# Attention's scores moved to earlier steps, and five of eight units per layer turned by DMA into the room of their own probabilities

## The chip, the core and the metric

The kernel runs on one core of one Trainium2 chip. A core has five engines with a queue of instructions each: PE (matrix products), ACT (activation functions, copies and casts), DVE (elementwise work and reductions), POOL, and SP, which here issues transfers. An instruction starts when those ahead of it in its queue have started and the semaphores that it waits for have come. Transfers run on 16 DMA engines. The metric is the device time of one execution in microseconds (us), as a median of runs.

## The reference

A trunk of two layers over 512 positions of width 1024, in float32. Each layer is a gated feed-forward (inner width 2816), a mixing stage, and a second feed-forward; a last norm follows. The change lies in the mixing stage:

```python
h = rms_norm(x, mix_norm[l])
z = h @ w_in[l]                                   # -> q | k | v | conv_B | conv_C | conv_h
attn_out = sliding_window_attention(q, k, v, attn_sink[l])
conv_out = short_conv(conv_B, conv_C, conv_h, conv_w[l])
x = x + jnp.concatenate([attn_out, conv_out], axis=-1) @ w_out[l]
```

Attention has 8 query heads of 64 in two groups that share a key and a value head. A block of 128 queries sees its own block of keys and the one before; a distance bias is added, and each head has a learned sink:

```python
scores = scores + bias[None, None]
scores = jnp.where(mask_b, scores, -jnp.inf)
m = jnp.maximum(jnp.max(scores, axis=-1, keepdims=True), sink_l)
p = jnp.where(mask_b, jnp.exp(scores - m), 0.0)
denom = jnp.sum(p, axis=-1, keepdims=True) + jnp.exp(sink_l - m)
out = jnp.einsum("bnkgqs,bnskd->bnqkgd", (p / denom), v_band)
```

## The kernel before

**Float32 by halves.** A float32 operand is split into a high and a low part (`hi`, `lo`): ACT casts the number to a shorter format, DVE subtracts that from the number. A product is three PE passes: high by high, low by high, high by low (L314 to L317). Feed-forward and output projection use a scheme with seven products in place of eight (`Seven`, matmuls at L941).

**Weights.** They come in pieces of 128x1024 (`raw`, eight rooms), loaded by SP's queue (L206), some with further pieces added to them by POOL's (L217, L278). ACT casts `wh` (L222) and DVE subtracts `wl` (L223), each with four rooms, three pieces ahead of PE (`SPLIT_AHEAD`); the load is called for four pieces ahead of the split (`LOAD_AHEAD`).

**The mixing stage.** Keys, values and the first two heads of `q` come from three products in halves of the positions (L350). Then fifteen whole products of 24 matmuls follow, each 128 columns of `w_in` by all 512 positions: three for `q` (two heads each), twelve for the convolution. `attend(step)` is called behind each one: the step is `2 + j` in the loop over `q`, so that step 3 is behind the first whole product, and goes on to 17 in `go_on`. In it, stages of attention stand that the tables at the top of the kernel give to this step.

**Attention's units.** There are eight per layer: block n of 4 by group g of 2, in the tables in the order (0,0), (1,0), (2,0), (3,0), (0,1), (1,1), (2,1), (3,1). A unit has four heads, and goes through these stages:

- `scores` (L1544, L1545 on PE; DVE adds the bias and takes the maximum, L1548; ACT takes the exponential, L1565, with the sink's in `es`, L1568; DVE scales by the sum, L1573). `p` is 128 queries by 4 x 256 keys, in a room of the weights' eight (`stock`). Units of n = 0 have only 128 keys.
- The probabilities must be turned, keys to partitions. `turn` does it on PE, four 128x128 transposes per block of keys (L1623), split from PSUM by ACT (L1626) and DVE (L1627).
- The other way is by DMA, for a unit with an entry in `SEND_AT`. DMA turns 16-bit elements, so `apart` has ACT copy the upper and the lower 16 bits of `p` into two planes (L1588, two copies of 128x1024), `send` has SP turn each plane (L1595), and `join` has ACT put the halves together again (L1608, two copies); ACT and DVE then split as above (L1612, L1614). Before, this is the way of units (1,0), (3,0) and (1,1), and `join` writes into `p` from a room of four planes, in `g8` or `xf`.
- `values` (L1638, L1639): PE multiplies by the values `vv`; ACT copies the upper half of the partitions (`ol`, L1641) and DVE adds the two into `mixed[0]` (L1644).

**Order.** A scheduler of the language places each engine's instructions by its own estimates of time. What it does to the order stands in the program: each engine runs its list as it is, and PE can't pass an instruction that waits. The rooms (`raw` 8, `g8` 4, `xf` 8, `g2` 11, PSUM `sc` 2, `aux` 2, `mm` 4) are reused as they come free, and a later user waits for the last reader.

Of the kernel before, what the change touches and what calls it, by code (L numbers as in the profile page):

```python
# [8 lines left out]
F32 = mybir.dt.float32  # L9
# [3 lines left out]
U16 = mybir.dt.uint16  # L13
# [3 lines left out]
P = 128  # L17
# [7 lines left out]
KC = D // P  # L25
NT = S // P
# [14 lines left out]
LAST = INNER[:-1] + (("d", (9, 10)),)  # L41
FORMS = ("a11", "a12", "s2", "s3", "s1", "a22", "s4")
EARLY = ("a11", "a12", "s3", "s2", "a22", "s1", "s4")
SCORES_AT = (5, 6, 7, 8, 9, 10, 12, 13)
TURN_AT = (6, None, 8, None, 11, None, 14, 15)
SEND_AT = (None, 7, None, 9, None, 11, None, None)
JOIN_AT = (None, None, None, None, None, 14, None, None)
LATE_JOIN_AT = (None, 10, None, 12, None, None, None, None)
VALUES_AT = (7, 11, 9, 13, 12, 15, 15, 16)
WARM = 3  # L50
XT_TAGS = ("sc", "aux", "aux", "mm", "sc", "sc", "aux", "aux")

# [24 lines left out]
def trunk_kernel(  # L77
# [23 lines left out]
    nc = tc.nc  # L101
# [3 lines left out]
    xpool = ctx.enter_context(tc.tile_pool(name="xpool", bufs=1))  # L105
# [7 lines left out]
    def g2(name, dt=F32, shape=(P, S)):  # L113
        return work.tile(list(shape), dt, tag="g2", bufs=11, name=name)

    def g8(name, dt=F32R, shape=(P, 2, 2, S)):
        return work.tile(list(shape), dt, tag="g8", bufs=4, name=name)
# [23 lines left out]
    def f32(ap):  # L141
        return ap.bitcast(F32)
# [576 lines left out]
    class Seven:  # L719
# [7 lines left out]
        def make(self, *names):  # L727
            for what in names:
                if what in self.forms:
                    continue  # L730
                hi, lo = both(f"f{what}_{self.name}")
                self.forms[what] = (hi, lo)
                b11, b12, b21, b22 = (
                    self.full[j][:, :, t * H : (t + 1) * H] for j in range(2) for t in range(2)
                )
                if what in ("t2", "t3") and not self.sums:
                    self.sums = self.room(self.name)
                    nc.vector.tensor_sub(self.sums[0], b12, b22)
# [748 lines left out]
    def mix(l, norm, after):  # L1487
        q = [None] * NH
# [35 lines left out]
        class Unit:  # L1524


            def __init__(self, n, g):
                self.n, self.g = n, g
                self.far = SEND_AT[NT * g + n]
                self.name = f"{l}_{n}_{g}"  # L1530
# [45 lines left out]

            def apart(self):

                if n_of(self) % NT == 1:
                    self.room = g8(f"pr_{self.name}", U16, (P, 4, KC * P))  # L1580
                else:
                    self.room = xpool.tile(
                        [P, 4, KC * P], U16, tag="xf", bufs=8, name=f"pr_{self.name}"
                    )
                src = self.p.bitcast(U16).rearrange("p h (b k z) -> p z h b k", b=2, z=2)
                with tc.issue_after(state["cast"].ins):
                    for z in range(2):
                        nc.scalar.copy(  # L1588
                            self.room[:, z].rearrange("p (b h k) -> p h b k", b=2, h=4), src[:, z]
                        )  # L1590

            def send(self):
                with tc.issue_after(state["load"].ins):
                    for z in range(2):
                        nc.sync.dma_start_transpose(  # L1595
                            self.room[:, 2 + z].rearrange("p (g q) -> p g q", q=P), self.room[:, z]
                        )

            def join(self):

                dst = self.p.bitcast(U16).rearrange("p h (k z) -> p z (h k)", z=2)
                turned = self.p.rearrange("p h k -> p (h k)").rearrange(
                    "p (b h q) -> p b h q", b=2, h=4
                )
                self.pt = []
                with tc.issue_after(state["cast"].ins):
                    for z in range(2):
                        nc.scalar.copy(dst[:, z], self.room[:, 2 + z])  # L1608
                for kb in range(2):
                    hi = g2(f"ph_{self.name}_{kb}", F32R, (P, 4, P))  # L1610
                    lo = g2(f"pl_{self.name}_{kb}", F32R, (P, 4, P))
                    nc.scalar.copy(hi, turned[:, kb])  # L1612
                    with tc.issue_after(state["sub"].ins):
                        nc.vector.tensor_sub(lo, turned[:, kb], f32(hi))  # L1614
                    self.pt.append((kb, hi, lo))
# [31 lines left out]

        todo = [Unit(n, g) for g in range(NKV) for n in range(NT)]

        def n_of(unit):  # L1650
            return NT * unit.g + unit.n

        def attend(step, what=(VALUES_AT, JOIN_AT, TURN_AT, SEND_AT, SCORES_AT)):

            stages = {VALUES_AT: "values", TURN_AT: "turn", SEND_AT: "send", SCORES_AT: "scores"}
            done = None
            for at in what:
                for unit, own in zip(todo, at):
                    if own == step:
                        done = getattr(unit, stages.get(at, "join"))() or done  # L1660
            return done

        for j in range(NH // 2):
# [3 lines left out]
            if j % 2 == 0:  # L1667
                room = both(f"q_{l}_{j}", shape=(P, 2, 2, S))
# [10 lines left out]
        step = 6  # L1679
# [4 lines left out]
        def go_on():  # L1684

            nonlocal step
            last = attend(step)
            step += 1
            with tc.issue_after(last.ins) if last else nullcontext():
                need_split(state["group"] - 1 + SPLIT_AHEAD)  # L1690
            attend(step - 1, (LATE_JOIN_AT,))

        for pair in range(2):
            cs = []
# [73 lines left out]
```

## Time and profile before

| | |
|---|---|
| median of 3 runs | 1641.39 us (1641.3 to 1644.91) |
| profiled execution | 1641.66 us, its span 1639.9 us |
| PE busy | 1629.8 us, 99% of the span |
| DVE, ACT, POOL busy | 1300.8, 1128.7, 193.5 us |
| mixing stage of layer 1, first whole product to first product of the output projection | 358.76 to 459.23 us |
| the 64 transposes of `p` on PE (L1623) | 270 to 329 ns each, the median 272 |

How to read it: times are from the start of the span. A row of the timeline gives start, duration, engine, line, operation, what is written and read, shape and count; in brackets the idle time before it and who ended it. Matmuls are pipelined, so the distance from one start to the next tells what a matmul takes of PE, and its duration, which is longer, does not. A row of the groups gives busy time and mean nanoseconds of one, then the idle time before. In a row of the windows, each engine's busy time in that stretch stands with its count of instructions.

### The profile page before, as it was taken

The page shows a single profiled execution, that of the slowest core. Times are in us where ns is not written, and L with a number is a line of the kernel's source. Part 1 is how long each engine was busy: PE and PEld are TensorE (multiplying, and loading weights), DVE is VectorE, ACT ScalarE, POOL GpSimd, SP SyncE. Part 2 cuts the span into 40 slices and gives each one's busy share as a digit, 9 for nine tenths or more (in the row PEclk, how much of TensorE's full clock was granted, in tenths as well). Part 3 has the DMA queues.
Part 4 walks back from the last instruction along what each step waited for, and adds up shares of the span by engine and source line. Part 5 has one row for each costly group of instructions (what it writes and reads, how often), then busy time and mean ns, then how long its engine had stood idle before and what let it go on. Part 6 is the DMA issues. An engine that isn't in the chain of part 4 may idle for free.

```text
span 1639.9 us, 21080 instructions
## 1 busy us (share of the span) xinstructions
PE 1629.8 (99%) x7576; PEld 1356.7 (83%) x7576; DVE 1300.8 (79%) x1718; ACT 1128.7 (69%) x1581; POOL 193.5 (12%) x172
## 2 busy tenths in 40 slices
PE   9999999999999999999999999999999999999998
PEld 7888888888888888888888888888988888888886
DVE  7987779877799867798788677896578987768895
ACT  7457777556867667786576777865587775777864
POOL 0011111100111111112001111110002101111111
PEclk9999999999999999999999999999999999999999
DMA  9379999932685788999837898996137857999991
GB/s 257 86 196 219 225 215 256 221 93 58 167 205 129 205 205 206 218 228 248 231 78 204 207 218 220 232 250 194 53 90 167 208 131 191 213 224 223 227 263 65
DMA packets 286844, 308.64 MB, mean 188 GB/s; under 512 B 108532, under 2 KB 171028, under 8 KB 286740
## 3 DMA queue, kind: packets, MB, share of 16 engines
q1 hardware_dynamic: 244212, 227.99, 47.8%
q0 software_dynamic: 41824, 78.65, 28.1%
q8 instruction: 59, 0.97, 0.2%
q10 hardware_dynamic: 704, 0.66, 0.1%
q14 instruction: 45, 0.37, 0.1%
HBM read 263.74 MB, written 2.10 MB: 162 GB/s over the span
## 4 chain that ended last, share of the span: by engine, by line
PE 92%; DVE 4%; ACT 1%; DMA 1%; issue 1%; SPq 0%; ACTq 0%; DVEq 0%
PE x L941 25%; PE y L941 13%; PE x_s L941 10%; PE w L941 6%; PE y_s L941 5%; PE down L373 3%; PE acc L314 3%; PE acc L315 3%; PE acc L317 3%; PE up L1097 3%; PE w_s L941 3%; PE acc L350 2%; DVE wl L223 1%; PE acc L839 1%; DMA raw<-in_w_out_dram 1%
## 5 line engine op out<-in xcount | busy, mean ns | idle before, releaser
L223 DVE TENSOR_TENSOR wl<-raw,wh 128x1024 fp32r<-128x1024 f32 (+1 forms) x493 | 596.2, 1214 | 219.9 <-ACT wh L222 216.7
L222 ACT CAST wh<-raw 128x1024 fp32r<-128x1024 f32 (+1 forms) x493 | 513.2, 1046 | 312.2 <-PE y L941 41.6
L941 PE MATMUL y<-wh,ft 128*128 128x512 f32 x608 | 187.3, 389 | 0.0
L941 PE MATMUL x<-wh,fb 128*128 128x512 f32 x608 | 187.3, 389 | 0.0
L941 PE MATMUL x<-wh,ft 128*128 128x512 f32 x608 | 187.3, 389 | 0.0
L941 PEld LDWEIGHTS x<-wh,ft 128*128 128x128 f32 x608 | 114.1, 188 | 23.7
L941 PEld LDWEIGHTS x<-wh,fb 128*128 128x128 f32 x608 | 114.1, 188 | 23.7
L941 PEld LDWEIGHTS y<-wh,ft 128*128 128x128 f32 x608 | 114.1, 188 | 23.7
L941 PE MATMUL y<-wl,ft 128*128 128x512 f32 x304 | 118.3, 389 | 0.0
L941 PE MATMUL x<-wl,fb 128*128 128x512 f32 x304 | 118.3, 389 | 0.0
L941 PE MATMUL x<-wl,ft 128*128 128x512 f32 x304 | 118.3, 389 | 0.0
L217 POOL DMA_DIRECT2D raw<-in_ffn_wu_dram x39 | 47.3, 1222 | 544.3 <-DMA raw<-in_ffn_wu_dram 327.0
L1266 ACT COPY raw_a<-pt 128x1024 uint16<-128x1024 uint16 x76 | 103.2, 1358 | 11.1 <-DMA pt<-pl 11.1
L314 PE MATMUL acc<-hh,wh 128*128 128x512 f32 x240 | 94.7, 394 | 0.0
L315 PE MATMUL acc<-hl,wh 128*128 128x512 f32 x240 | 93.8, 391 | 0.0
L317 PE MATMUL acc<-hh,wl 128*128 128x512 f32 x240 | 93.7, 391 | 0.0
L941 PE MATMUL w<-wh,fb 128*128 128x512 f32 x304 | 93.6, 389 | 0.0
L941 PE MATMUL x_s<-wh,ft_s 128*128 128x512 f32 x256 | 78.8, 389 | 0.0
L941 PE MATMUL y_s<-wh,ft_s 128*128 128x512 f32 x256 | 78.8, 389 | 0.0
L250 DVE TENSOR_TENSOR raw<-raw,raw 128x1024 f32<-128x1024 f32 x58 | 70.6, 1222 | 7.1 <-DMA raw<-in_ffn_wd_dram 5.9
L217 POOL DMA_DIRECT2D raw<-in_ffn_wg_dram x39 | 47.1, 1212 | 233.7 <-DVE u L1250 62.3
L941 PE MATMUL x_s<-wh,fb_s 128*128 128x512 f32 x240 | 73.9, 389 | 0.0
(364 smaller groups left out, 3421.3 us busy)
## 6 DMA issues: line engine op xcount, KB each, us to landing
raw<-in_ffn_wu_dram SPq DMA_DIRECT2D x120, 512.0 KB, 5.2
raw<-in_ffn_wd_dram SPq DMA_DIRECT2D x104, 512.0 KB, 6.3
raw<-in_ffn_wg_dram SPq DMA_DIRECT2D x80, 512.0 KB, 4.9
raw<-in_ffn_wu_dram POOLq DMA_DIRECT2D x39, 512.0 KB, 8.1
raw<-in_ffn_wg_dram POOLq DMA_DIRECT2D x39, 512.0 KB, 6.0
raw<-in_w_in_dram SPq DMA_DIRECT2D x36, 512.0 KB, 4.3
raw<-in_ffn_wd_dram POOLq DMA_DIRECT2D x32, 512.0 KB, 8.5
raw<-raw POOLq DMA_DIRECT2D x20, 512.0 KB, 8.5
```

What stands on the lines that cost most here:

```text
L217: nc.gpsimd.dma_start(out=r, in_=rows_of(*more), accum_op=ALU.add)
L222: cast = nc.scalar.copy(hi, raw)
L223: state["sub"] = eng.tensor_sub(lo, raw, f32(hi))
L250: nc.vector.tensor_add(a11, a11, s1)
L314: nc.tensor.matmul(acc, hi[:, k, :], rhs[k][0], start=k == first, stop=False)
L315: nc.tensor.matmul(acc, hi[:, k, :], rhs[k][1], start=False, stop=False)
L317: nc.tensor.matmul(acc, lo[:, k, :], rhs[k][0], start=False, stop=k == last)
L350: nc.tensor.matmul(accs[j][:, t * H : (t + 1) * H], w[:, k, :], x_, start=t + k + i == 0, stop=k == KC - 1 and i == 2, skip_group_check=True,)
L373: nc.tensor.matmul(acc, a[:, k, tok], w[:, k, :], start=i + k + n == 0 and fresh[t], stop=i == last and k == 1 and n == 2, skip_group_chec ...
L941: nc.tensor.matmul(accs[u], x_[:, 2 * h + k, tok], w[:, k, :], start=start and h + k + i == 0, stop=h + k == 2 and i == 2, skip_group_chec ...
L1097: nc.tensor.matmul(accs[t], x_[:, tok], w[:, k, :], start=j + k + i == 0, stop=j == 3 and k == 1 and i == 2,)
L1266: nc.scalar.copy(room.rearrange("p c (n z) -> p c z n", z=2)[:, :, z, :], turned[0][:, NT * z + 2 * c : NT * z + 2 * c + 2, :],)
```

## The change

Two things change, in the same way in both layers.

**When.** Scores move from steps 5, 6, 7, 8, 9, 10, 12, 13 to 3, 4, 5, 6, 8, 7, 9, 11, so that unit (1,1) now goes ahead of (0,1). Turning, sending, joining and `values` move with them. There is one table for `join` in place of two, and a join stands behind the call for the next weight split of its step.

**How.** Units (2,0) and (2,1) also go by DMA, so that only (0,0), (0,1) and (3,1) are turned on PE. The four planes become two (`planes`): `apart` writes into them, `send` turns them into the room of `p` itself (`back`), and `join` writes from there into the planes, where the split then reads. Four units share two rooms by halves, one of `g8` and one of `xf`; the fifth takes a room of the weights' eight.

```diff
-SCORES_AT = (5, 6, 7, 8, 9, 10, 12, 13)
-TURN_AT = (6, None, 8, None, 11, None, 14, 15)
-SEND_AT = (None, 7, None, 9, None, 11, None, None)
-JOIN_AT = (None, None, None, None, None, 14, None, None)
-LATE_JOIN_AT = (None, 10, None, 12, None, None, None, None)
-VALUES_AT = (7, 11, 9, 13, 12, 15, 15, 16)
+SCORES_AT = (3, 4, 5, 6, 8, 7, 9, 11)
+TURN_AT = (4, None, None, None, 10, None, None, 13)
+SEND_AT = (None, 5, 6, 7, None, 8, 10, None)
+JOIN_AT = (None, 8, 9, 10, None, 11, 13, None)
+VALUES_AT = (6, 9, 10, 11, 12, 12, 14, 15)
...
             def apart(self):
-                if n_of(self) % NT == 1:
-                    self.room = g8(f"pr_{self.name}", U16, (P, 4, KC * P))
-                else:
-                    self.room = xpool.tile(
-                        [P, 4, KC * P], U16, tag="xf", bufs=8, name=f"pr_{self.name}"
-                    )
                 src = self.p.bitcast(U16).rearrange("p h (b k z) -> p z h b k", b=2, z=2)
+                self.planes = rooms.pop(0)()
                 with tc.issue_after(state["cast"].ins):
                     for z in range(2):
                         nc.scalar.copy(
-                            self.room[:, z].rearrange("p (b h k) -> p h b k", b=2, h=4), src[:, z]
+                            self.planes[:, z].rearrange("p (b h k) -> p h b k", b=2, h=4), src[:, z]
                         )
             def send(self):
+                self.back = self.p.rearrange("p h k -> p (h k)").bitcast(U16)
+                self.back = self.back.rearrange("p (z n) -> p z n", z=2)
                 with tc.issue_after(state["load"].ins):
                     for z in range(2):
                         nc.sync.dma_start_transpose(
-                            self.room[:, 2 + z].rearrange("p (g q) -> p g q", q=P), self.room[:, z]
+                            self.back[:, z].rearrange("p (g q) -> p g q", q=P), self.planes[:, z]
                         )
             def join(self):
-                dst = self.p.bitcast(U16).rearrange("p h (k z) -> p z (h k)", z=2)
+                whole_ = self.planes.rearrange("p z n -> p (z n)")
+                dst = whole_.rearrange("p (n z) -> p z n", z=2)
+                turned = whole_.bitcast(F32).rearrange("p (b h q) -> p b h q", b=2, h=4)
                 self.pt = []
                 with tc.issue_after(state["cast"].ins):
                     for z in range(2):
-                        nc.scalar.copy(dst[:, z], self.room[:, 2 + z])
+                        nc.scalar.copy(dst[:, z], self.back[:, z])
...
+        rooms = [half_of(f"pr_{l}_0", h, in_g8) for h in range(2)]
+        rooms += [half_of(f"pr_{l}_1", h, in_xf) for h in range(2)]
+        rooms.append(lambda: stock(f"pr_{l}_2", U16, (P, 2, KC * P)))
...
-            attend(step - 1, (LATE_JOIN_AT,))
+            attend(step - 1, (JOIN_AT,))
```

The order that the scheduler then gives, in the same way in both layers. On PE the scores of unit (0,0) stand behind and within the first two whole products, its transposes within the third; the output products of (1,0), (2,0) and (3,0) stand ahead of and among the matmuls of the eighth, ninth and tenth. On ACT the copies that part, the copies that join and the casts of five units lie between the third product and the end of the eleventh, with the casts of the weights between them. On SP the turns of a unit stand between the loads of `w_in`, as before, now five pairs in place of three.

More of the change, by code (lines that the diff above doesn't have):

```diff
@@ L1595, in send @@
                         nc.sync.dma_start_transpose(
-                            self.room[:, 2 + z].rearrange("p (g q) -> p g q", q=P), self.room[:, z]
+                            self.back[:, z].rearrange("p (g q) -> p g q", q=P), self.planes[:, z]
                         )
             def join(self):
-                dst = self.p.bitcast(U16).rearrange("p h (k z) -> p z (h k)", z=2)
-                turned = self.p.rearrange("p h k -> p (h k)").rearrange(
-                    "p (b h q) -> p b h q", b=2, h=4
-                )
+                whole_ = self.planes.rearrange("p z n -> p (z n)")
+                dst = whole_.rearrange("p (n z) -> p z n", z=2)
+                turned = whole_.bitcast(F32).rearrange("p (b h q) -> p b h q", b=2, h=4)
                 self.pt = []
@@ L1648, in mix, with half_of, room, in_g8 @@
         todo = [Unit(n, g) for g in range(NKV) for n in range(NT)]
-        def n_of(unit):
-            return NT * unit.g + unit.n
-        def attend(step, what=(VALUES_AT, JOIN_AT, TURN_AT, SEND_AT, SCORES_AT)):
+        shared_rooms = {}
+        def half_of(name, half, make):
+            def room():
+                if not half:
+                    shared_rooms[name] = make(name)
+                return shared_rooms[name][:, half]
+            return room
+        def in_g8(name):
+            return g8(name, U16, (P, 2, 2, KC * P))
+        def in_xf(name):
+            return xpool.tile([P, 2, 2, KC * P], U16, tag="xf", bufs=8, name=name)
+        rooms = [half_of(f"pr_{l}_0", h, in_g8) for h in range(2)]
+        rooms += [half_of(f"pr_{l}_1", h, in_xf) for h in range(2)]
+        rooms.append(lambda: stock(f"pr_{l}_2", U16, (P, 2, KC * P)))
+        def attend(step, what=(VALUES_AT, TURN_AT, SEND_AT, SCORES_AT)):
             stages = {VALUES_AT: "values", TURN_AT: "turn", SEND_AT: "send", SCORES_AT: "scores"}
```

## The prediction

> **What bounds the kernel now.** I read the page first, then the waits of the output products of attention, then the mixing stage of layer 1 cut into windows, then its groups by shape and its timeline.
>
> ```profile
> PE 1629.8 (99%) x7576; PEld 1356.7 (83%) x7576; DVE 1300.8 (79%) x1718; ACT 1128.7 (69%) x1581; POOL 193.5 (12%) x172
> ...
> PE 92%; DVE 4%; ACT 1%; DMA 1%; issue 1%; SPq 0%; ACTq 0%; DVEq 0%
> ...
>   DVE pl L1627: 1.0, 2
>   DVE pl L1614: 0.4, 2
> ...
> core 0: us, PE busy (x) PEld busy (x) DVE busy (x) ACT busy (x) POOL busy (x), PEclk, DMA share, GB/s
> 358.76:377.00 18.24, 18.24 (x89) 15.27 (x88) 9.96 (x13) 11.80 (x18) 0.00 (x0) 1.00 0.20 58
> 377.00:390.00 13.00, 13.00 (x67) 10.77 (x66) 10.67 (x38) 9.01 (x26) 0.00 (x0) 1.00 0.15 42
> 390.00:405.00 15.00, 15.00 (x82) 12.69 (x81) 12.04 (x36) 10.51 (x22) 1.29 (x1) 1.00 0.39 93
> 405.00:420.00 15.00, 15.00 (x73) 12.52 (x73) 11.85 (x46) 14.66 (x37) 1.30 (x1) 1.00 0.47 117
> 420.00:435.00 15.00, 15.00 (x75) 12.56 (x74) 11.36 (x31) 14.66 (x25) 1.22 (x1) 1.00 0.59 144
> 435.00:447.00 12.00, 12.00 (x64) 10.09 (x62) 9.86 (x23) 7.53 (x17) 2.78 (x2) 1.00 0.74 168
> 447.00:459.23 12.23, 12.18 (x56) 9.77 (x54) 10.69 (x16) 6.11 (x10) 3.69 (x3) 1.00 0.91 217
> ```
>
> PE is busy for 99% of the span and carries 92% of the chain, so the time changes in two ways only: PE gets less to do, or PE is made to wait. In attention the output products' second halves (L1639) are what PE still waits at: 1.4 us in four places of two layers, for DVE. The windows show what covers the rest: ACT, off the chain over the whole run, is full from 405 to 435 (14.66 of 15.00, twice) and has spare time before and behind. This is where the change puts more on ACT. Layer 2 runs the same instructions in the same order, so I work one layer and double it.
>
> **What PE is spared.** Two more units per layer (unit 2 of both groups of heads) are turned by DMA, so 2 x 8 transposes leave PE; units (0,0), (0,1) and (3,1) keep 4 + 4 + 8.
>
> ```profile
> 358.76 0.40 PE L314 MATMUL acc<-hh,wh 128*128 128x512 f32 x1
> ...
> 430.63 0.39 PE L1638 MATMUL o<-ph,vv 128*128 128x512 f32 x1
> ...
> 431.62 0.28 PE L1544 MATMUL sc<-k,q 128*128 128x256 f32 x1
> ...
> 432.58 0.40 PE L314 MATMUL acc<-hh,wh 128*128 128x512 f32 x1
> ...
> 438.05 1.04 PE L1623 MATMUL pt<-ident,p 128*128 128x128 f32 x8
> 438.85 0.48 PE L314 MATMUL acc<-hh,wh 128*128 128x512 f32 x1
> ...
> 452.99 0.39 PE L1638 MATMUL o<-ph,vv 128*128 128x512 f32 x1
> 453.43 0.50 PE L1639 MATMUL o<-pl,vv 128*128 128x512 f32 x1
> 453.76 0.40 PE L314 MATMUL acc<-hh,wh 128*128 128x512 f32 x1
> ```
>
> The pitch counts, not the duration: eight transposes take 438.85 - 438.05 = 0.80 us and hold up the next matmul some 0.1, so 16 of them are 1.8 us. A whole product (24 matmuls) takes 438.05 - 432.58 = 5.47, 0.228 a matmul; a unit's scores 432.58 - 431.62 = 0.96 (0.9 for unit 0, whose are half as wide); four output matmuls 431.62 - 430.63 = 0.99. The waits at L1639 delay PE by less than their 0.7 a layer: at the last one the matmuls stand 0.44 and 0.33 apart in place of 0.23, 0.3 lost, some 0.4 with the other. Those halves now come earlier, so that goes too. In all 2.2 us a layer are spared: 4.4 in the program, if nothing else happened.
>
> The Trainium skill (VectorE: DVE Perf Modes, "The three transpose paths") gives a 128x128 transpose 390 ns on TensorE and 1309 ns by the DMA crossbar, and under its rules says to use TensorE where PSUM will do as destination, which speaks against this change. Taken as PE's price, 390 ns would make the spared 16 an estimated 6.2 us a layer in place of 1.8; the pitch of 0.10 above decides.
>
> **What ACT gets in exchange.** For each of the two units: two copies that part the halves (L1588), two that join them (L1608), and two casts from SBUF (L1612) in place of two from PSUM (L1626).
>
> ```profile
> L222 ACT CAST wh<-raw 128x1024 fp32r<-128x1024 f32 x16 | 16.8, 1052 | 14.1 <-PE acc L315 14.1
> L1608 ACT COPY p<-pr 128x1024 uint16<-128x1024 uint16 x6 | 7.9, 1361 | 0.0
> L1588 ACT COPY pr<-p 128x1024 uint16<-128x1024 uint16 x6 | 6.0, 1045 | 0.0
> L1626 ACT CAST ph<-pt 128x512 fp32r<-128x512 f32 x8 | 4.5, 589 | 1.1 <-PE pt L1623 1.1
> L1612 ACT CAST ph<-p 128x512 fp32r<-128x512 f32 x6 | 3.5, 622 | 0.0
> L1706 ACT ACTIVATE cc<-ch,par 128x512 f32<-128x512 f32 x4 | 2.9, 723 | 1.7 <-DVE ch L1704 1.7
> ...
> 391.17 2.00 ACT L1588 COPY pr<-p 128x1024 uint16<-128x1024 uint16 x2
> 393.07 0.51 ACT L1565 ACTIVATE p<-p,nm 128x256 f32<-128x256 f32 x1
> ...
> 395.05 0.20 ACT L1568 ACTIVATE es<-es 128x4 f32<-128x4 f32 x1
> ...
> 411.16 0.40 ACT L1565 ACTIVATE p<-p,nm 128x128 f32<-128x128 f32 x1
> ...
> 412.71 0.20 ACT L1568 ACTIVATE es<-es 128x4 f32<-128x4 f32 x1
> ...
> 422.44 2.59 ACT L1608 COPY p<-pr 128x1024 uint16<-128x1024 uint16 x2
> 424.89 1.05 ACT L222 CAST wh<-raw 128x1024 fp32r<-128x1024 f32 x1
> ```
>
> Back to back, ACT's instructions overlap by about 0.1: a pair that parts is 1.90, a pair that joins 2.45, a unit's exponentials with `es` 2.08 (1.65 for unit 0), a weight cast 0.95, a 512-wide cast or copy 0.50, `cc` and `tap` together 1.26. So ACT gets 2 x (1.90 + 2.45) = 8.7 us a layer on 74.28 of 100.47 (the windows summed): 83 of 98. On average it has room; what counts is where.
>
> The Trainium skill (ScalarE: Activation LUTs, "What ACT_TABLE_LOAD costs") has ACT take one element per cycle at any width, 186 + 0.833 N ns: an estimated 1039 ns for both copies. The parting copy agrees (1045), the joining one does not (1361), and the row decides.
>
> **Where PE meets ACT.** The fifteen whole products of the stage are P1 (358.76) to P15; step k follows P(k-2). Scores now follow P1 to P7 and P9; the output products of units (1,0), (2,0), (3,0) follow P7, P8 and P9, and stand in PE's order among the matmuls of P8 to P10. PE cannot pass them.
>
> *After P1.* Unit 0's scores need all of the first four heads, which before were long done.
>
> ```profile
> 366.67 0.68 DVE L1672 SCALAR_TENSOR_TENSOR q<-acc,q 64x512 fp32r<-64x512 f32 x1
> 368.01 0.69 DVE L1672 SCALAR_TENSOR_TENSOR q<-acc,q 64x512 fp32r<-64x512 f32 x1 [0.66 <-ACT q L1671]
> ...
> L1548 DVE CUSTOM_DVE_ANT_0 p<-sc,bias,sink 128x256 f32<-128x256 f32 x24 | 10.7, 477 | 0.5 <-PE sc L1545 0.5
> L1573 DVE TENSOR_SCALAR p<-p,sums 128x256 f32<-128x256 f32 x24 | 6.8, 351 | 0.1
> ```
>
> Heads 2 and 3 end at 367.35 and 368.70. PE would have P1, half the scores and nine matmuls of P2 behind it at 358.76 + 5.47 + 0.45 + 2.05 = 366.7 and waits 0.65; after half the scores of the next pair and four more matmuls it waits 0.2 again. Unit 0's transposes inside P3 and its output after the values' own turn (vv) wait for DVE: 0.3 in all. Together 1.1.
>
> *Output of (1,0).* ACT waits last before it parts unit (1,0). For that P3 must be done and unit 2's scores begun, at 358.76 + 16.4 + 0.9 + 0.96 + 0.45 + 0.35 + 1.0 of waits = 378.8; then, after 0.5 of scores, DVE runs three reductions, a head and the four scalings (3 x 0.48 + 0.69 + 4 x 0.35 = 3.5): 382.8. In ACT's order there follow, up to the second cast of (1,0): four pairs that part (7.60), one that joins (2.45), three wide exponentials and one narrow (7.9), three weight casts (2.85), five 512-wide copies (2.5), `cc` and `tap` (1.26), 24.6 in all: it starts at 407.4 and is done at 408.0. PE is there after seven products (38.3), five wide and two narrow scores (6.6), transposes and vv (0.8), five single matmuls (1.1) and the waits so far (1.1): 406.7. Wait 1.3.
>
> *Output of (2,0).* ACT goes on with the join, a weight cast, `cc`/`tap`, `ol`, exponentials: 7.7, cast done at 415.7. PE resumes at 408.0 and has 23 matmuls, two outputs, four transposes and scores: 415.1. Wait 0.6, and 0.2 for DVE's other half.
>
> *Output of (3,0).* ACT: half a join, two casts, a pair that parts, `ol`, a cast, half a join, a weight cast: 7.3 more, done at 423.0. PE: four outputs and P9's 24 matmuls, 422.3. Wait 0.7 and 0.15.
>
> After that nothing: (1,1) is cast before PE gets there, (2,1) and (3,1) by some 5 us, since ACT has time again from about 440.
>
> Sum of waits: 1.1 + 1.3 + 0.8 + 0.85 = 4.05, say 4.2 with the pipeline's bubbles. Net 4.2 - 2.2 = +2.0 a layer, +4.0 in the program.
>
> **What I cost at nothing.** The weight casts stay far ahead: P12's, the one named in the sum for (3,0), starts at about 421 and P12 not before 438; were that cover gone, each us by which ACT is late would be one of PE's. SP issues two more pairs per layer:
>
> ```profile
> 392.25 2.63 SPq L1595 DMA_TRANSPOSE pr<-pr  x2
> ...
> DMA to landing us min/median/max: 3.1/3.2/3.3
> ```
>
> 2.63 of issue and 3.2 to landing against 12 us from parting to joining of unit (1,0) in the sums above (384.7 to 396.5), and more for the others. Behind waiting transposes stand weight loads in SP's order (the load for P11 behind those of (1,0), for P12 behind those of (3,0)), used 20 us later. Loads now wait for ACT's joins where p's rooms come free, P15's for the join of (3,0) at about 422, with P15 not before 455. Two `cc` additions on POOL now stand behind a DMA-adding of weights each: up to 4 us late, needed a product later. The new rooms (p itself; shared planes) change no instruction's size.
>
> **The sum.** The profiled execution took 1641.66 us (span 1639.9), 0.27 above the median of the three, 1641.39. 1641.66 + 4.0 = 1645.7. Bounds: no waits at all, 1641.66 - 4.4 = 1637.3. ACT 5% dearer than the rows over its 40 full us is 2 late at the end, and PE with it: +4.0 a layer, 1649.7; with 1 us a layer more of bubbles, where outputs stand among a product's matmuls, 1651.7.
>
> **Rivals.** *ACT arrives in time* (not slower): if ACT reaches that cast of (1,0) 1.3 us sooner, 5% of the 24.6, waits on ACT vanish, 1.1 of early ones stay: 1641.66 + 2 x (1.1 - 2.2) = 1639.5. For it: before 405 ACT is idle for 15 us in the windows. Against it: those gaps are waits for DVE and PE, and the order is fixed. *ACT is later than the rows say*: the 5% above, 1649.7. For it, each dependent copy or cast also pays its start, which back-to-back rows don't show; against it, most of these copies did stand back to back in the rows I took. *The DMA turns come late*: three pairs within 15 us on SP; a join that waits 3 us for its landing would add 6: 1651.7. Against it the 12 us of room.
>
> By the skill's 1039 ns for a joining copy, ACT would gain 0.6 a pair, some 1.8 of the 4.2 would go, and the time would be an estimated 1642; six copies of just that form took 1361 here, so I give it no chance of its own.
>
> **How the numbers follow.** Forecast (waits of 3 to 5.5 us a layer, 1643 to 1648.5): 0.58. ACT in time: 0.17. ACT later: 0.16. DMA late, or something that I don't see: 0.06. A gain past PE's 4.4: 0.03. About 0.3%, 4.9 us, is what a measurement of this kernel tells from no change. It lies at 1646.3, inside the forecast's own range and a little above its middle, so the forecast gives 0.33 to within and 0.25 to slower; ACT in time 0.16 to within and 0.01 to faster; the next two are slower, the last is faster. Within 0.49, slower 0.47, faster 0.04. Range 1639 to 1651.
>
> **What would show it.** Right: PE's waits get ACT `ph` before the output products, 3 to 6 us in all, and DVE `q` before the scores, 1 to 2; ACT over 98% busy from 385 to 430; 32 transposes left. Wrong: no wait for `ph`; or waits for `wh` or `wl` at L314 to L317; or ACT idle for a DMA before it joins.

## The result and the profile after

The changed kernel takes 1646.9 us (median of 8 runs, 1646.57 to 1647.45) against 1641.35 us of the kernel before, measured beside it: a ratio of 1.0032, 95% interval 1.0021 to 1.0043. It is slower by 5.5 us. The forecast was 1645.7 us, with a range of 1639 to 1651. The profiled execution took 1646.82 us, its span 1645.0, which is 5.1 us more than before.

All of these 5.1 us lie in the mixing stage: from the first whole product to the first product of the output projection it is 103.07 us in layer 1 and 103.10 us in layer 2 (before 100.47 and 100.46), 2 x 2.6 us more. The rest of the program, which is the span less the two stages, took 1438.8 us, and 1439.0 us before. Line numbers after the tables are one to a few less than before: the transposes on PE are L1618 now, the parting copies L1582, the joining copies L1603, the casts and differences of joined units L1607 and L1609, the output products L1633 and L1634.

From the page of the changed kernel, busy times and the shares of the chain:

```profile
PE 1629.6 (99%) x7544; PEld 1352.9 (82%) x7544; DVE 1299.4 (79%) x1718; ACT 1142.0 (69%) x1597; POOL 195.1 (12%) x172
...
PE 86%; ACT 6%; DVE 5%; DMA 1%; issue 1%; SPq 0%; ACTq 0%; DVEq 0%
```

PE has 32 matmuls fewer (7544 in place of 7576), and still its busy time is the same to 0.2 us, as a matmul that has waited shows a longer duration (0.50 us in place of 0.39 in the rows below) and waits too short for the view count as busy. ACT's share of the chain is 6% where it was 1%. The waits of PE (in all us, times, longest) have a new first row:

```profile
PE o L1633 <- ACT ph L1607: 4.6, 6, 1.3
```

Six waits, three in each layer, for ACT's casts. The windows of layer 1 show where:

```profile
390.00:405.00 15.00, 15.00 (x75) 12.69 (x74) 10.73 (x40) 14.98 (x28) 0.68 (x1) 1.00 0.73 172
405.00:420.00 15.00, 13.29 (x66) 10.59 (x66) 10.20 (x31) 14.98 (x33) 3.42 (x2) 1.00 0.31 73
420.00:435.00 15.00, 14.43 (x64) 11.40 (x63) 13.77 (x33) 14.83 (x26) 0.00 (x0) 1.00 0.65 175
...
385.00:430.00 45.00, 42.68 (x204) 34.59 (x204) 34.78 (x112) 44.78 (x91) 4.10 (x2) 1.00 0.57 130
```

ACT (the fourth figure behind the length) is busy for 44.78 of the 45 us from 385 to 430, and PE, which was full there before, loses 1.7 us from 405 to 420 and 0.6 from 420 to 435. In the timeline, these are the three outputs with what stands around them:

```profile
358.87 0.40 PE L313 MATMUL acc<-hh,wh 128*128 128x512 f32 x1
...
406.92 0.39 PE L313 MATMUL acc<-hh,wh 128*128 128x512 f32 x1
407.91 0.61 ACT L1607 CAST ph<-pr 128x512 fp32r<-128x512 f32 x1
408.57 0.50 PE L1633 MATMUL o<-ph,vv 128*128 128x512 f32 x1 [1.26 <-ACT ph L1607]
408.91 0.40 PE L314 MATMUL acc<-hl,wh 128*128 128x512 f32 x1
...
415.64 0.28 PE L1544 MATMUL sc<-k,q 128*128 128x256 f32 x1
415.72 0.60 ACT L1607 CAST ph<-pr 128x512 fp32r<-128x512 f32 x1
416.37 0.50 PE L1633 MATMUL o<-ph,vv 128*128 128x512 f32 x1 [0.45 <-ACT ph L1607]
...
422.84 0.39 PE L316 MATMUL acc<-hh,wl 128*128 128x512 f32 x1
423.13 0.61 ACT L1607 CAST ph<-pr 128x512 fp32r<-128x512 f32 x1
423.80 0.50 PE L1633 MATMUL o<-ph,vv 128*128 128x512 f32 x1 [0.57 <-ACT ph L1607]
...
461.94 0.62 PE L940 MATMUL x_m<-wh,fb_m 128*128 128x512 f32 x2
```

The distance from start to start tells what a wait costs. At (1,0) the output stands 408.57 - 406.92 = 1.65 us behind its predecessor in place of 0.23: 1.42 us. At (2,0) it is 0.61 (0.73 in place of 0.12), at (3,0) 0.73 (0.96 in place of 0.23). Each time PE goes on 0.06 us or less after ACT's cast has ended (407.91 + 0.61 = 408.52), and each time the next matmul is late too: 408.91 - 408.57 = 0.34 in place of 0.23, 0.11 more.

### The profile page after: what moved, and what is told of

Read it like the earlier page. It is cut to its first block, busy times and chain, and to the rows that moved or that the text cites. A ratio compares the mean times of both kernels' runs of the same rounds, so it can differ in the third digit from the quotient of the medians.

```text
span 1645.0 us, 21048 instructions
## 1 busy us (share of the span) xinstructions
PE 1629.6 (99%) x7544; PEld 1352.9 (82%) x7544; DVE 1299.4 (79%) x1718; ACT 1142.0 (69%) x1597; POOL 195.1 (12%) x172
## 4 chain that ended last, share of the span: by engine, by line
PE 86%; ACT 6%; DVE 5%; DMA 1%; issue 1%; SPq 0%; ACTq 0%; DVEq 0%
PE x L940 25%; PE y L940 13%; PE x_s L940 10%; PE w L940 6%; PE y_s L940 5%; PE down L372 3%; PE up L1096 3%; PE acc L313 2%; PE acc L314 2%; PE acc L316 2%; PE w_s L940 2%; PE acc L349 2%; DVE wl L222 2%; ACT p L1564 1%; ACT pr L1582 1%
## 5 line engine op out<-in xcount | busy, mean ns | idle before, releaser
L940 PE MATMUL x<-wh,fb 128*128 128x512 f32 x608 | 187.2, 389 | 0.0
L940 PE MATMUL x<-wh,ft 128*128 128x512 f32 x608 | 187.2, 389 | 0.0
L940 PE MATMUL y<-wh,ft 128*128 128x512 f32 x608 | 187.2, 389 | 0.0
L940 PEld LDWEIGHTS x<-wh,fb 128*128 128x128 f32 x608 | 114.1, 188 | 23.7
L940 PEld LDWEIGHTS x<-wh,ft 128*128 128x128 f32 x608 | 114.1, 188 | 23.7
L940 PEld LDWEIGHTS y<-wh,ft 128*128 128x128 f32 x608 | 114.1, 188 | 23.7
L940 PE MATMUL x<-wl,fb 128*128 128x512 f32 x304 | 118.3, 389 | 0.0
L940 PE MATMUL x<-wl,ft 128*128 128x512 f32 x304 | 118.3, 389 | 0.0
L940 PE MATMUL y<-wl,ft 128*128 128x512 f32 x304 | 118.3, 389 | 0.0
L940 PE MATMUL w<-wh,fb 128*128 128x512 f32 x304 | 93.6, 389 | 0.0
L940 PE MATMUL x_s<-wh,ft_s 128*128 128x512 f32 x256 | 78.8, 389 | 0.0
L940 PE MATMUL y_s<-wh,ft_s 128*128 128x512 f32 x256 | 78.8, 389 | 0.0
L940 PE MATMUL x_s<-wh,fb_s 128*128 128x512 f32 x240 | 73.9, 389 | 0.0
```

The lines of the kernel that those rows point to most:

```text
L940: nc.tensor.matmul(accs[u], x_[:, 2 * h + k, tok], w[:, k, :], start=start and h + k + i == 0, stop=h + k == 2 and i == 2, skip_group_chec ...
```

## The experiments

Edits are shown against the changed kernel. The stage is the yardstick: its length repeats from layer 1 to layer 2 within 0.07 us in all but the last two runs, while whole times also hold waits for loads elsewhere that differ from execution to execution (one of 1.5 us for `wl` at L940, far ahead of the stage, stands in the trace of the first experiment). The ratios are to the kernel before, run beside each: it took 1642.94 us beside e1 to e4, 1641.66 beside e5 to e8, 1641.93 beside e9 and e10 and 1641.74 beside e11, so ratios and stages compare better than times of different rows.

| run | stage, layer 1 | stage, layer 2 | time, us | ratio, 95% interval |
|---|---|---|---|---|
| before | 100.47 | 100.46 | 1641.35 | 1 |
| changed | 103.07 | 103.10 | 1646.9 | 1.0032 (1.0021 to 1.0043) |
| e1, outputs a product later | 100.46 | 100.45 | 1642.21 | 0.9998 (0.9989 to 1.0006) |
| e2, three units by DMA | 103.43 | 103.46 | 1649.32 | 1.0039 (1.0026 to 1.0051) |
| e3, five by DMA, steps of before | 102.19 | 102.20 | 1648.74 | 1.0038 (1.0026 to 1.0050) |
| e4, rooms alone | 101.22 | 101.23 | 1643.62 | 1.0009 (0.9998 to 1.0021) |
| e5, (1,0) joined sooner | 103.09 | 103.13 | 1648.7 | 1.0042 (1.0029 to 1.0056) |
| e6, rooms and early scores | 102.06 | 102.13 | 1645.98 | 1.0025 (1.0015 to 1.0035) |
| e7, joins on DVE | 102.82 | 102.85 | 1647.84 | 1.0035 (1.0023 to 1.0047) |
| e8, outputs later still | 99.04 | 99.03 | 1640.01 | 0.9990 (0.9981 to 0.9999) |
| e9, e8 with three by DMA | 100.78 | 100.79 | 1642.57 | 1.0004 (0.9996 to 1.0013) |
| e10, one join copy more | 106.45 | 107.98 | 1653.95 | 1.0069 (1.0053 to 1.0084) |
| e11, e8 with six by DMA | 101.41 | 111.41 | 1655.1 | 1.0081 (1.0064 to 1.0099) |

### e1: the outputs a product later

```diff
-VALUES_AT = (6, 9, 10, 11, 12, 12, 14, 15)
+VALUES_AT = (6, 10, 11, 12, 12, 13, 15, 15)
```

> Only the table of the outputs changes against the changed kernel: (1,0), (2,0), (3,0), (1,1) and (2,1) have their output products one product (5.5 us) later, all else at its step. Theory 1 (ACT reaches the casts of the joined units 0.6 to 1.5 us after PE): the three waits for ph go, 1.42 + 0.61 + 0.73 and some 0.7 of pieces around them, 3.4 us a layer; stage of layer 1 about 99.6 us in place of 103.07, time 1640 (1639 to 1641.5), and no PE wait for ph in first place. Rival 2 (the time is lost through the turns on SP's queue or the new rooms): a product more of room doesn't touch that, 1645 to 1647. Rival 3 (ACT is short of time as such): the waits move one product back and stay, 1644 to 1647.

The three waits are gone, and the stage is back at 100.45 us, 2.65 less. They neither stayed (rival 2) nor moved a product back (rival 3). That is the way of theory 1, but 0.85 short of its sum, and the time is above the 1641.5 that it allowed, as two other waits came in their place:

```profile
429.78 0.47 PE L313 MATMUL acc<-hh,wh 128*128 128x512 f32 x1 [0.27 <-DVE m L1639]
...
435.69 0.50 PE L1633 MATMUL o<-ph,vv 128*128 128x512 f32 x1 [0.19 <-ACT cc L1708]
```

By distances, these cost 0.43 and 0.35 us, with 0.08 and 0.11 behind them. The first is a wait for the accumulator that an output's second half still held.

### e2: the new steps, three units by DMA

```diff
-TURN_AT = (4, None, None, None, 10, None, None, 13)
-SEND_AT = (None, 5, 6, 7, None, 8, 10, None)
-JOIN_AT = (None, 8, 9, 10, None, 11, 13, None)
+TURN_AT = (4, None, 7, None, 10, None, 11, 13)
+SEND_AT = (None, 5, None, 7, None, 8, None, None)
+JOIN_AT = (None, 8, None, 10, None, 11, None, None)
```

> The changed kernel's times, but units (2,0) and (2,1) turned on PE again: 16 transposes a layer back on PE (+1.8), 8.7 us a layer off ACT, two pairs of turns off SP. Theory 1, in the form that ACT's amount of work makes the waits: the waits for ph at (2,0) and (3,0) go (1.8 with their pieces) and that at (1,0) shrinks by the part of its queue that goes, net some -0.5 to -1.5 a layer, 1644 to 1646. In the form that the order on ACT makes them: the wait at (1,0) stays whole, since ACT still has the parting of (1,1) and the exponentials of (0,1) ahead of the second cast of (1,0), the other two go: +1.8 - 1.8 - the rest = 0, 1646.5 to 1647.5. Rival 2 (DMA turns late): the gain of fewer turns shows as waits that go altogether, below 1644.

The waits at (2,0) and (3,0) went, one at (1,0) stayed (1.51 us for the first of the two casts, 0.51 for DVE's difference behind it; in the changed kernel it was the second cast that PE waited for), and the stage is 0.36 longer: the form of the theory in which the order on ACT counts. ACT had less to do (73.8 us in the stage in place of 82.0), and its casts for (1,0) came no sooner:

```profile
401.13 1.05 ACT L221 CAST wh<-raw 128x1024 fp32r<-128x1024 f32 x1
402.08 0.72 ACT L1717 ACTIVATE cc<-ch,par 128x512 f32<-128x512 f32 x1
402.70 1.98 ACT L1582 COPY pr<-p 128x1024 uint16<-128x1024 uint16 x2
...
406.84 0.61 ACT L1607 CAST ph<-pr 128x512 fp32r<-128x512 f32 x1
407.35 1.05 ACT L221 CAST wh<-raw 128x1024 fp32r<-128x1024 f32 x1
408.30 0.62 ACT L1607 CAST ph<-pr 128x512 fp32r<-128x512 f32 x1
```

The scheduler filled what was freed with the casts of unit (2,0) from PSUM (at 394.73 and 396.15) and with a fourth weight cast (at 407.35, between the two casts of (1,0)). The first cast of (1,0) starts at 406.84, against 402.91 in the changed kernel, the second at 408.30 against 407.91. PE meanwhile got there sooner, as the scores of (2,1) now stand behind this output. So less work on ACT alone didn't help: what stands ahead of the cast that PE needs next is what counts.

### e3, e4 and e6: the parts one by one

e4 has the new rooms and joins with the steps and the three units of before. e6 is e4 with the first two units' scores early. e3 has the scores of before (but for unit (2,1)) with five units by DMA.

```diff
 # e4
+SCORES_AT = (5, 6, 7, 8, 9, 10, 12, 13)
+TURN_AT = (6, None, 8, None, 11, None, 14, 15)
+SEND_AT = (None, 7, None, 9, None, 11, None, None)
+JOIN_AT = (None, 10, None, 12, None, 14, None, None)
+VALUES_AT = (7, 11, 9, 13, 12, 15, 15, 16)
 # e6: e4 with
+SCORES_AT = (3, 4, 7, 8, 9, 10, 12, 13)
+TURN_AT = (4, None, 8, None, 11, None, 14, 15)
+SEND_AT = (None, 5, None, 9, None, 11, None, None)
+VALUES_AT = (6, 11, 9, 13, 12, 15, 15, 16)
 # e3
+SCORES_AT = (5, 6, 7, 8, 9, 10, 11, 13)
+TURN_AT = (6, None, None, None, 11, None, None, 15)
+SEND_AT = (None, 7, 8, 9, None, 11, 12, None)
+JOIN_AT = (None, 10, 11, 12, None, 14, 15, None)
+VALUES_AT = (7, 11, 12, 13, 12, 15, 16, 16)
```

> The steps of before and three units by DMA as before, only with the new rooms (turned into the room of p, joined into the planes) and with the joins behind the call for the weight split. Theory 1: nothing changes but the place of a join, 1641 to 1643.5. Rival 2 (rooms shared by halves, loads that wait for joins): 1644 or more.

> The kernel with only new rooms and the steps of before, of which the scores of the first two units alone go to steps 3 and 4 (unit (0,0) turned at 4 and multiplied at 6, unit (1,0) sent at 5, its join and output where they were). Theory 1: only the early waits for q appear, 0.6 us before scores and some 0.5 in pieces, stage 101.2 + 1.1 = 102.3 us. If early scores are not what costs, 101.2 to 101.5; if they push DVE or ACT back for the whole stage, 103 or more.

> The other half of the change alone: scores, turns and outputs at the steps of before (unit (2,1)'s scores one step sooner, the outputs of (2,0) three, of (2,1) one step later than before), but five units by DMA in the new rooms. Theory 1 (what counts is where ACT's work meets PE's outputs): the 1.8 us a layer of transposes is gained, early waits for q don't occur, and waits at outputs are less than in the changed kernel as ACT is free till 390: 1640 to 1644. If the two additional units by themselves are the cost, whatever the step: 1645 to 1648.

e4 is 0.77 us a layer longer than before, and one row holds it: `PE o L1634 <- DVE pl L1609`, 1.5 us in two places, one in each layer at the output of (1,1), whose join now stands behind the call for the weight split. By distances it is 0.88, with two restarts of 0.11, and the 0.3 that was lost before at the output of (2,1) (at 453.43) is gone. The rooms themselves show no wait. e6 adds 0.9 us to that, in the places that the prediction named (0.18, 0.31 and 0.14 ahead of scores, the rest in pieces): the early scores cost 0.9 a layer and disturb nothing behind. e3 is a miss of the expectation. Five units at the old steps don't gain the 1.8, they lose as much: output products wait for `ph` and `pl` in eight places of 0.1 to 0.64 us a layer. Each join stands one step ahead of its outputs; so it did before for three units, where PE lost next to nothing by it, and whether one step more would take them away at these steps was not run. By its time alone e3 is nearer to the rival (two additional units cost, whatever the step); e8 and e9 below speak against it, where the same two units gain. The span of its trace is 8.0 us over that of before, of which the stage explains 3.5; 2.8 us are waits for `wh` at L940 outside the stage (0.2 to 1.3 in the other traces), and whether these belong to the edit was not settled.

### e5: (1,0) joined a step sooner

```diff
-JOIN_AT = (None, 8, 9, 10, None, 11, 13, None)
+JOIN_AT = (None, 7, 9, 10, None, 11, 13, None)
```

> The changed kernel with one number other: unit (1,0) is joined a step sooner (7 in place of 8). On ACT its two casts then stand ahead of the parting of (1,1), of the exponentials of (0,1) and of a cc and tap. If ACT is behind by the sum of its work (theory 1, as a backlog), putting one unit first only moves the wait: 1.42 at (1,0) goes, about 2 stands at (2,0), the sum of PE's waits for ph and the stage (103.1 us) stay within 0.4. If ACT's order at (1,0) alone is the cause (theory 1b, for which the run with three units by DMA speaks), some 1.5 a layer goes and nothing comes: stage 101.6. If the turns by DMA are late (rival 2), the join waits for its landing, as it has a product less, and ACT stands idle before it.

The wait moved, as a backlog would have it. First the row of the waits, then PE in the timeline at the output of (2,0):

```profile
PE o L1633 <- ACT ph L1607: 5.6, 4, 1.9
```

```profile
412.44 0.36 PE L1543 MATMUL sc<-k,q 128*128 128x256 f32 x1
414.70 0.50 PE L1633 MATMUL o<-ph,vv 128*128 128x512 f32 x1 [1.90 <-ACT ph L1607]
415.04 0.39 PE L313 MATMUL acc<-hh,wh 128*128 128x512 f32 x1
```

Nothing at (1,0), 2.14 us at (2,0), 1.05 at (3,0), the stage within 0.03. No time was won by serving one unit first, which speaks for the backlog and against the order at (1,0) alone; and ACT did not stand idle ahead of a join, so the turns were there in time with a product less of room.

### e7: the joins on DVE

```diff
-                with tc.issue_after(state["cast"].ins):
+                with tc.issue_after(state["sub"].ins):
                     for z in range(2):
-                        nc.scalar.copy(dst[:, z], self.back[:, z])
+                        nc.vector.tensor_copy(dst[:, z], self.back[:, z])
```

> The changed kernel with the ten joining copies of a layer on DVE in place of ACT; ACT is spared 12.3 us a layer. Theory 1: at the price of ACT (1361 ns) DVE, busy for 11 to 12 of 15 us in this stretch, becomes the late one and PE waits for pl in place of ph, stage 105 to 108 us; at half of that price or less the waits for ph shrink to under 1 us a layer and the stage is 100.5 to 102. Rival 2 (DMA): no change in either, 103.

The price is between the two of the expectation, and so is the stage, 102.85 us. The copy takes 750 ns on DVE (least, median, most) where ACT takes 1361, and then the waits are for DVE:

```profile
L1603 DVE COPY pr<-p x20: 726/750/769, 398.5 to 1255.3; 128x1024 uint16<-128x1024 uint16 x20
```

```profile
PE o L1634 <- DVE pl L1609: 2.5, 2, 1.2
...
PE o L1633 <- ACT ph L1607: 1.0, 2, 0.5
```

ACT spared 12.3 us a layer and the stage gained 0.25: the lateness went over to the engine that took the work.

### e8 and e9: outputs later, and what the turning is then worth

```diff
 # e8
-TURN_AT = (4, None, None, None, 10, None, None, 13)
+TURN_AT = (5, None, None, None, 10, None, None, 13)
-VALUES_AT = (6, 9, 10, 11, 12, 12, 14, 15)
+VALUES_AT = (7, 10, 11, 13, 12, 14, 15, 16)
 # e9: e8 with
+TURN_AT = (5, None, 7, None, 10, None, 11, 13)
+SEND_AT = (None, 5, None, 7, None, 8, None, None)
+JOIN_AT = (None, 8, None, 10, None, 11, None, None)
```

> The first run's idea carried further: outputs of (0,0), (1,0) one product later than in the changed kernel, (2,0) one, (3,0) and (1,1) two, (2,1) and (3,1) one, and unit (0,0) turned a product later; scores, turns by DMA and joins as in the changed kernel. Theory 1: no wait for ph or for m is left, only the early ones for q (about 0.9 us a layer with their pieces); with 1.8 spared on PE the stage is 99.3 to 99.8 us against 100.47 before, the time some 1.5 to 2.3 us under that of before. Rival (other waits come in their place as at 429.78 and 435.69 in the first run): 100.2 or more.

> The run with the outputs carried further, but units (2,0) and (2,1) turned on PE again. Where no output waits, the transposes are left as the only difference on PE. If they cost their pitch (the step of the prediction, 16 x 0.10 and some holding up): +1.8 us a layer, stage 100.8 in place of 99.03, the time 3.6 us more. If a transpose cost its latency of 0.27 us or more: +4.3 or more, stage 103.3. If ACT's time were still what counts: no more than 0.5.

e8 beats both kernels: a stage of 99.03 us, 1.43 under before and 4.07 under the changed kernel, and 1640.01 us (ratio 0.9990, interval 0.9981 to 0.9999, so its lead on the kernel before is small). The stage is 0.3 below the expected range; the wait at the output of (0,0), 0.3 in the changed kernel (shown further down), is gone too. Its windows and one output:

```profile
405.00:420.00 15.00, 15.00 (x76) 12.65 (x75) 12.02 (x33) 14.98 (x33) 1.68 (x1) 1.00 0.42 96
420.00:435.00 15.00, 15.00 (x72) 12.50 (x71) 12.05 (x29) 14.93 (x25) 0.44 (x1) 1.00 0.65 175
```

```profile
407.83 0.61 ACT L1607 CAST ph<-pr 128x512 fp32r<-128x512 f32 x1
...
411.39 0.39 PE L1633 MATMUL o<-ph,vv 128*128 128x512 f32 x1
```

ACT is as full as in the changed kernel (14.98 and 14.93 of 15.00), and PE loses nothing: the second cast of (1,0) ends at 408.44 (there 408.52), and PE asks for it at 411.39 in place of 407.15. An engine at 100% that nobody waits for cost nothing here.

e9 differs from e8 by the two units alone, and is 1.74 and 1.76 us longer in the two layers: 16 transposes on PE at their pitch (1.6) and some 0.1 where a product goes on behind them. The prediction had 1.8. So turning two units by DMA is worth 3.5 us in the program where the outputs stand late enough, and 0.7 (103.46 against 103.10, twice) where they don't.

### e10: one joining copy twice

```diff
-                    for z in range(2):
+                    for z in (0, 0, 1) if self.n == 1 and self.g == 0 else range(2):
```

> The changed kernel with one joining copy done twice for unit (1,0): 1.23 us more on ACT at about 404, nothing else asked of anyone. If ACT's backlog makes the waits (theory 1), all that it delivers later is later by 1.2 and PE with it: the sum of waits at the three outputs, 2.76 a layer, grows by 1.2 or, as the order on ACT shifts too, by up to 2.5; stage 104.3 to 105.6. If ACT had slack there: 103.1 to 103.4.

The waits at the three outputs grew from 2.76 to 1.88 + 0.44 + 2.66 = 4.98 us, 2.2 more, at the upper end of what was expected. The stage went past it, to 106.45 and 107.98, for a reason that nobody had expected. Here is PE at the output of (3,0), and the granted clock (third figure from the end) in that stretch:

```profile
424.15 0.28 PE L1544 MATMUL sc<-k,q 128*128 128x256 f32 x1
426.94 0.80 PE L1633 MATMUL o<-ph,vv 128*128 128x512 f32 x1 [2.50 <-ACT ph L1607]
427.53 0.63 PE L313 MATMUL acc<-hh,wh 128*128 128x512 f32 x1
427.95 0.63 PE L314 MATMUL acc<-hl,wh 128*128 128x512 f32 x1
```

```profile
427.00:430.00 3.00, 3.00 (x8) 2.41 (x9) 2.67 (x8) 2.55 (x3) 0.00 (x0) 0.53 0.61 104
430.00:435.00 5.00, 5.00 (x23) 4.11 (x22) 3.54 (x11) 3.07 (x10) 0.00 (x0) 1.00 0.21 82
```

After 2.5 us without work PE's clock is 0.53, and matmuls stand 0.43 us apart in place of 0.23: seven of them in layer 1 (some 1.5 us lost) and fourteen in layer 2 (some 3.0). Without this, both stages are 105.0, inside the expectation. A wait of 1.90 us did not do it (e5, the rows above: 0.34 and then 0.23 again). The trace is of the slowest of the four executions (1652.24 to 1656.41 us), so the loss by the clock need not be as large in each.

### e11: six units by DMA

```diff
 # e8 with
+TURN_AT = (5, None, None, None, 10, None, None, None)
+SEND_AT = (None, 5, 6, 7, None, 8, 10, 12)
+JOIN_AT = (None, 8, 9, 10, None, 11, 13, 14)
+        rooms.append(lambda: in_g8(f"pr_{l}_3")[:, 0])
```

> The run with the outputs carried further, and unit (3,1) by DMA too (sent at 12, joined at 14, output at 16 as it was; its planes in a room of g8): six units, and of the 32 transposes left in the program 16 more go. On PE 0.9 us a layer less; on ACT 4.4 more, in a stretch (420 to 447) where it was no longer full all the time. If turning by DMA is free as long as no output catches up with ACT (theory 1): stage 98.1 to 98.5 in place of 99.03, the time 1.2 to 1.8 us less. If ACT's work itself costs: 99.0 or more.

Both theories fail here. In layer 2 the rival that had found no support so far is the cause: the turn comes late. In layer 1 it is the larger part; ahead of it 0.54 us are lost at 433.67, where PE waits for ACT's copy `cc` (0.44 by the distance and 0.10 behind it). PE's waits, ACT's and SP's queues in layer 2, and the landing of turns (the last figure, median us) from 1247 to 1254 and, for comparison, from 380 to 432:

```profile
PE o L1633 <- ACT ph L1607: 10.3, 2, 9.6
```

```profile
1239.98 7.19 SPq L205 DMA_DIRECT2D raw<-in_w_out_dram  x4
1247.44 5.82 SPq L1591 DMA_TRANSPOSE p<-pr  x2
...
1252.56 0.62 ACT L1607 CAST ph<-pr 128x512 fp32r<-128x512 f32 x1
1253.37 15.95 SPq L205 DMA_DIRECT2D raw<-in_w_out_dram  x4
1265.86 1.33 ACT L1603 COPY pr<-p 128x1024 uint16<-128x1024 uint16 x1 [12.68 <-DMA p<-pr]
```

```profile
p<-pr SPq DMA_TRANSPOSE x2, 16.6
...
p<-pr SPq DMA_TRANSPOSE x10, 3.3
```

Ten turns earlier in layer 1 land in 3.3 us. The sixth unit's stand behind four loads of `w_out` on SP while POOL adds more weights by DMA, and land in 8.1 us in layer 1 and 16.6 in layer 2; ACT, with time in hand, stands idle 3.77 and 12.68 us ahead of the join, PE 0.87 and 9.75. In layer 1 some 1.7 us more follow at DVE's `pl` and `ch` behind the late join; in layer 2 PE's matmuls stand 0.43 us apart for 5 us behind the wait, at this clock:

```profile
1267.70:1273.05 5.35, 5.34 (x12) 3.72 (x12) 4.43 (x7) 5.29 (x8) 1.12 (x1) 0.50 0.71 225
```

Why layer 2 is twice as slow as layer 1 was not tried, nor which of the two, the loads ahead on SP or POOL's beside them, makes the turn late. The DMA engines' share was 0.91 and more while it was under way, and 0.44 and 0.64 from 405 to 435. So a turn by DMA was hidden when it was issued at 423 us or sooner, as the changed kernel's last one is (420.00), and not at 435.5, behind the loads for the output projection.

## Why the prediction was right

The time came out 1.2 us above the forecast and inside its range; the sign and the mechanism hold, as shown by e1, e8 and e9. Term by term, a layer:

| step of the prediction | forecast | measured | from |
|---|---|---|---|
| 16 transposes off PE | -1.8 | -1.76 | e9 less e8 |
| waits at L1639 gone | -0.4 | -0.3 | distances before, at 453.43 and 453.76 |
| early scores, transposes, vv | 1.1 | 0.9 | e6 less e4 |
| output of (0,0), for vv | in the 1.1 | 0.3 | 0.20 and 0.11 at 386 |
| output of (1,0) | 1.3 | 1.53 | 1.42 and 0.11 |
| output of (2,0) | 0.6 + 0.2 | 0.83 | 0.61 and twice 0.11 |
| output of (3,0) | 0.7 + 0.15 | 0.95 | 0.73 and twice 0.11 |
| outputs behind it | 0 | 0.2 | 0.09 and 0.11 at 444 |
| net | +2.0 | +2.6 | the stage |

The row of (0,0) is not in e6, where no wait stands at that output. In the changed kernel DVE ends `vv` at 386.50, and PE goes on behind it:

```profile
383.17 2.00 ACT L1582 COPY pr<-p 128x1024 uint16<-128x1024 uint16 x2 [0.58 <-DVE p L1572]
...
385.81 0.69 DVE L1520 TENSOR_TENSOR vv<-vp,vv 128x512 fp32r<-128x512 f32 x1
...
386.23 0.28 PE L1543 MATMUL sc<-k,q 128*128 128x256 f32 x1
386.55 0.19 PEld L1633 LDWEIGHTS o<-ph,vv 128*128 128x128 f32 x1 [0.25 <-DVE vv L1520]
386.55 0.50 PE L1633 MATMUL o<-ph,vv 128*128 128x512 f32 x1
386.89 0.40 PE L1634 MATMUL o<-pl,vv 128*128 128x512 f32 x1
```

- *ACT's queue.* The second cast of (1,0) was put at 407.4 and started at 407.91; that of (2,0) at 415.1 (done 415.7), and started at 415.72; that of (3,0) at 422.4 (done 423.0), and started at 423.13. PE was put at 406.7 for (1,0) and was there at 407.15. Both were half a microsecond late, so the wait came out right. Most of ACT's lateness was there at the start: the copies that part (1,0), its last wait, begin at 383.17 (first row above) in place of 382.8; the work from there to the second cast took 24.7 us, 24.6 by the sum. ACT's work in the stage, 83 us by the sum, is 82.0.
- *What was sized too small* is "the pipeline's bubbles", 0.15 in the sum. Behind seven matmuls of the outputs that waited, the next one is 0.11 us late as well: 0.8 us in the stage. The rows of the table add up to 2.65. The 0.6 by which the net was missed lies in several rows, most of it at (1,0), where a restart of 0.11 was not counted, and at the outputs behind (3,0), which were put at nothing. At (2,0) and (3,0) the 0.2 and 0.15 forecast for DVE's other half came out as two restarts of 0.11 each, one behind the long wait and one behind a short one (for DVE's `pl` at (2,0), for ACT's other cast at (3,0)), so the fit of these two is in part luck.
- *Costed at nothing*: weight casts were in time, as no product waits for `wh` or `wl` in the stage. The turns by DMA were in time in the changed kernel (no idle time of ACT ahead of a join), but e11 shows that "12 us of room" is not a general cover: the landing of 3.2 us did not hold where the DMA engines were nearly full (a share of 0.91 and more). The price given for this rival, 6 us, was too low for that case: e11 is 2.4 us longer than e8 in layer 1 and 12.4 in layer 2. The new rooms cost nothing by themselves (e4).
- *The price of a transpose.* The 390 ns that the prediction quotes is told for bf16 in the Trainium skill (VectorE: DVE Perf Modes, "The three transpose paths"). The float32 transposes here were worth 0.11 us each on PE (1.76 us for 16).
- *The signs.* 32 transposes left, ACT busy for 99.5% from 385 to 430, waits for `ph` of 4.6 us in all (3 to 6 forecast): as forecast. Waits for `q` of 1 to 2 us don't show as a row at all. They are in the distances (0.19, 0.29 and 0.14 ahead of scores, 0.6 a layer), below what the view counts as idle.
- *The rivals.* ACT in time did not happen, and e8 shows an order in which it does: PE asks for the second cast of (1,0) some 3 us after its end. ACT 5% dearer would have given 1649.7; from 383.17 to the second cast of (1,0) it was 0.1 us dearer in 24.6, under 1%.

## What to carry to other kernels

A busy share tells which engine can be late, not whether it costs: ACT was full in the changed kernel and just so in the version that is faster than both, and what differed was by how much its results preceded the one who needs them. When work is moved to another engine, move the consumers as well (here by one or two products of 5.5 us), and read the slack at each meeting point from two queues in the timeline; a place gained for one unit only moves the wait to the next (e5). A DMA in the path is priced by its landing in the stretch where it will be issued, not by a median over the run (3.3 us against 8 and 17).

## What was not expected of the hardware

PE's clock fell after a short idle time: with 2.50 and 2.53 us idle (e10) the granted clock was 0.53 behind it, matmuls stood 0.43 us apart in place of 0.23 (e11, behind 9.59 us idle, 0.43 too), and it took 2.7 us in layer 1 and 6.1 us in layer 2 to be back. With 1.90 us idle (e5, both layers) nothing of the kind is seen. Where between these the limit lies, and whether the waits of 1.7 us that PE had 18 us sooner in e10 count, no run shows. So a wait of 2.5 us, 2.7 by the distance of the starts, cost PE 4.1 and 5.7 in all. The Trainium skill (TensorE: Matmul & The Clock Gate, "What's actually happening") has the clock fall after an idle window of some 3.4 us and return after one such window of work, windows that run freely. The halved clock agrees; the idle time that was enough here is shorter, and the return took less in one case and more in the other.

The same copy that joins 16-bit halves takes 750 ns on DVE and 1361 ns on ACT (e7).
